# Way down of two of three lots of hidden tiles as seven block products, weight sums by adding transfers, and a third buffer for the second gate/up weight

## The chip, the cores and the metric

The kernel runs on one core of one Trainium2 chip. The metric is the device time of one execution in microseconds (us); the time before is the median of three runs, 1095.49 us (1094.43 to 1097.13). The engines of the core are TensorE (PE: matmuls, its weight loads shown as PEld), VectorE (DVE), ScalarE (ACT), GpSimd (POOL) and SyncE (SP, which issues transfers).

## The reference

Two transformer layers on x of 512 tokens x 1024, in fp32: a token mixer with memory attention, then a gated feed-forward part. The change touches the feed-forward part only:

```
h  = rms_norm(x, g_ffn_pre[i])
gu = h @ w_gate_up[i]                                    # 1024 x (2 * 2816)
f  = (silu(gu[..., :D_FF]) * gu[..., D_FF:]) @ w_down[i]  # 2816 x 1024
x  = x + rms_norm(f, g_ffn_post[i])
```

## The kernel before, in words

**Precision.** Every fp32 factor of a product is held as two numbers, a rounded high part (ACT copies it into the matmul format) and the low remainder (DVE subtracts), made by `split` (L313, L317). A product is then three matmuls: high x high, high x low, low x high (`mm3`, L303 to L305).

**Tiles and lots.** The 2816 hidden columns are 22 tiles of 128 (`NF`), the 512 tokens four row tiles (`NT`). `LOTS` (L44) groups the hidden tiles into three lots: eight, six and eight. For each lot the kernel first makes the hidden tiles (gate/up), then multiplies them with their rows of `w_down` (way down) and adds the result into `o`, four tiles of 128 x 1024 fp32. The third lot's way down is in `ffn_out`, together with the norm that ends the layer.

**Gate/up.** Hidden tiles 0 and 1 of a layer are made plainly (`plain`, `act`). Tiles 2 to 21 go through `body` (L1085): the 512 tokens and the 1024 inputs are halved, and gate and up stand for the two column halves, so that eight block products become seven (Strassen's scheme in Winograd's form). Each of the seven is `seven` (L1059): 4 x 3 matmuls of 256 columns. The token side's sums are made once per layer by `Forms`; the weight side's sums are made for every hidden tile: `prep_a` loads the first weight `ra` and splits it, `load_b` loads the second, `rb`, and makes two sums on DVE (L1043, L1044), `prep_c` makes the third (L1049) and splits `ru`, `prep_b` splits `rb`, `prep_d` adds once more (L1056) and splits 512 columns. Within a tile the products are S2, nS1, S3, S4, A22; the first two of the next tile (`p1`, `p2`: A11, A12) stand between them. DVE also combines the products (L1082, L1101, L1109), multiplies silu(gate) by up (L1115) and splits the hidden tile (L1117 on ACT, L1118 on DVE).

**Way down.** `down` (L896): for each half of 512 output columns and each unit of two hidden tiles, one weight load of 128 x 1024, one split, then 4 row tiles x 2 x 3 matmuls of 512 columns. The first unit's products of row tiles 0 and 1 are issued early, inside the last gate/up tile (`fill`, the functions `first` and `second`), to bridge the time in which that tile is finished. In layer 0 every unit also calls `ahead` (L226): two calls together load and split one weight of layer 1's mixer and store the two parts to memory (14 calls in all, of eight weights asked for).

**Order.** PE's order is the program's. The other engines' and the transfers' order is chosen by a scheduler from what is ready; instructions then run in that order on each engine. A buffer of a pool is handed on when its last reader is done: `raw` has three, `ru` and `rb` two each, the split weights `hi` and `lo` four each. PSUM has eight banks: `acc` two, `s0` to `s2`, `pv`, `t` two. Transfers are issued by SP.

```
LOTS = ((0, 8), (8, 14), (14, 22))
            ru, rb = [gu.tile([P, 1024], F32, tag=z, name=z, bufs=2) for z in ("ru", "rb")]
```

## Time and profile before

| | |
|---|---|
| median of three runs | 1095.49 us |
| profiled execution | 1097.01 us, its span 1094.9 us |
| granted TensorE clock | 0.998 of full |
| transfers | 142.44 MB, of which the queue of SP has 140.80 MB |
| layer 0, feed-forward by blocks | from 222 us to 549 us of the span |
| layer 1, the same | from 776 us to the end |

A row of the profile names a line of the kernel, the engine, the operation, what it writes and reads by the program's names, the shape, and then the busy time in all, the mean time of one in ns, and the idle time of the engine just before, with what ended it. Rows in order of time give the start, the duration, and in brackets an idle time and its end. Matmuls overlap in the pipeline: the duration of one in a row is longer than the distance to the next.

### The profile page before, as it was taken

How to read it: one execution, taken by the hardware profiler on the slowest of the kernel's cores; microseconds unless marked ns; L12 is line 12 of the kernel's file. 1: busy time of each engine (PE TensorE's matmuls, PEld its weight loads, DVE VectorE, ACT ScalarE, POOL GpSimd, SP SyncE). 2: the span in 40 equal slices, each digit the busy share in tenths (PEclk: the TensorE clock that was granted, in tenths of full speed). 3: DMA queues.
4: the chain of work that ended last, by engine and by line, in shares of the span. 5: the costliest groups of instructions: out<-in, count | busy, mean ns of one | idle time of the engine just before them, and what ended most of it. 6: DMA issues, size and time to landing. Idle time of an engine off the chain costs nothing.

```text
span 1094.9 us, 19518 instructions
## 1 busy us (share of the span) xinstructions
PE 1072.8 (98%) x7436; PEld 985.0 (90%) x7436; DVE 840.8 (77%) x1433; ACT 659.1 (60%) x1357; POOL 197.7 (18%) x341
## 2 busy tenths in 40 slices
PE   9999999999999999999999999999999999999997
PEld 7899878999889989998898888878999899899986
DVE  7889875999548867975888988758996478669854
ACT  7679874756445535653567888756664366346631
POOL 5773231102000000000444543312000000000001
PEclk9999999999999999999999999999999999999999
DMA  9621007344833472335533221144136123423243
GB/s 339 250 78 40 20 20 261 125 154 129 283 140 116 153 252 78 116 108 187 197 126 116 78 78 40 39 176 172 53 110 222 59 89 120 139 68 105 88 165 116
DMA packets 40702, 142.44 MB, mean 130 GB/s; under 512 B 4768, under 2 KB 5152, under 8 KB 40480
## 3 DMA queue, kind: packets, MB, share of 16 engines
q1 hardware_dynamic: 40320, 140.80, 37.4%
q8 instruction: 58, 0.95, 0.4%
q10 hardware_dynamic: 288, 0.40, 0.1%
q14 instruction: 36, 0.29, 0.1%
HBM read 122.30 MB, written 18.87 MB: 129 GB/s over the span
## 4 chain that ended last, share of the span: by engine, by line
PE 70%; DVE 5%; issue 2%; ACT 1%; POOL 1%; DMA 0%; DVEq 0%; POOLq 0%; ACTq 0%
PE ps L1065 11%; PE ps L1066 11%; PE ps L1067 11%; PE ps L304 10%; PE ps L303 10%; PE ps L305 10%; PE tp L668 2%; DVE wlo L317 1%; PE o L683 1%; PE o L682 1%; PE s L607 1%; PE s L608 1%; POOL r L337 1%; DVE hrows L317 1%; POOL p L658 0%
## 5 line engine op out<-in xcount | busy, mean ns | idle before, releaser
L313 ACT ACTIVATE whi<-raw 128x1024 fp32r<-128x1024 f32 (+3 forms) x206 | 169.2, 839 | 170.1 <-PE ps L1067 69.0
L317 DVE TENSOR_TENSOR wlo<-raw,whi 128x1024 fp32r<-128x1024 f32 (+3 forms) x202 | 191.0, 960 | 68.8 <-ACT whi L313 64.8
L1066 PE MATMUL ps<-hrows,wlo 128*128 128x256 f32 x640 | 176.4, 276 | 0.0
L1065 PE MATMUL ps<-hrows,whi 128*128 128x256 f32 x640 | 176.2, 275 | 0.0
L1067 PE MATMUL ps<-hrows,whi 128*128 128x256 f32 x640 | 176.2, 275 | 0.0
L303 PE MATMUL ps<-whi,hrows 128*128 128x256 f32 (+2 forms) x432 | 144.1, 333 | 0.0
L304 PE MATMUL ps<-wlo,hrows 128*128 128x256 f32 (+2 forms) x432 | 138.0, 320 | 1.6 <-DVE wlo L317 1.6
L304 PE MATMUL ps<-wlo,f 128*128 128x512 f32 (+1 forms) x360 | 138.6, 385 | 0.0
L303 PE MATMUL ps<-whi,f 128*128 128x512 f32 (+1 forms) x360 | 138.5, 385 | 0.0
L305 PE MATMUL ps<-whi,f 128*128 128x512 f32 (+1 forms) x360 | 138.5, 385 | 0.0
L305 PE MATMUL ps<-whi,hrows 128*128 128x256 f32 (+2 forms) x432 | 138.0, 320 | 0.0
L1065 PE MATMUL ps<-a,whi 128*128 128x256 f32 x480 | 132.3, 276 | 2.9 <-DVE c L1101 2.9
L1066 PE MATMUL ps<-a,wlo 128*128 128x256 f32 x480 | 132.1, 275 | 0.0
L1067 PE MATMUL ps<-a,whi 128*128 128x256 f32 x480 | 132.1, 275 | 0.0
L1066 PEld LDWEIGHTS ps<-hrows,wlo 128*128 128x128 f32 x640 | 120.1, 188 | 0.6
L1065 PEld LDWEIGHTS ps<-hrows,whi 128*128 128x128 f32 x640 | 120.1, 188 | 0.5
L1067 PEld LDWEIGHTS ps<-hrows,whi 128*128 128x128 f32 x640 | 120.1, 188 | 0.0
L346 POOL TENSOR_SCALAR e<-sso 128x1 f32<-128x1 f32 x8 | 3.4, 422 | 550.5 <-ACT junk L341 550.3
L658 POOL TENSOR_SCALAR p<-p,rd 128x256 f32<-128x256 f32 (+2 forms) x128 | 77.4, 623 | 102.5 <-DVE rd L655 62.3
L1065 PEld LDWEIGHTS ps<-a,whi 128*128 128x128 f32 x480 | 90.1, 188 | 3.5 <-DVE c L1101 3.3
L1066 PEld LDWEIGHTS ps<-a,wlo 128*128 128x128 f32 x480 | 90.1, 188 | 0.2
L1067 PEld LDWEIGHTS ps<-a,whi 128*128 128x128 f32 x480 | 90.1, 188 | 0.0
(201 smaller groups left out, 2551.0 us busy)
## 6 DMA issues: line engine op xcount, KB each, us to landing
raw<-in_wgu_dram SPq DMA_DIRECT2D x48, 512.0 KB, 4.4
raw<-in_wd_dram SPq DMA_DIRECT2D x44, 512.0 KB, 4.5
rb<-in_wgu_dram SPq DMA_DIRECT2D x40, 512.0 KB, 3.6
raw<-in_wo_dram SPq DMA_DIRECT2D x17, 512.0 KB, 4.1
raw<-in_wq_dram SPq DMA_DIRECT2D x16, 512.0 KB, 4.9
xt<-x SPq DMA_DIRECT2D x12, 512.0 KB, 4.9
raw<-in_wm_dram SPq DMA_DIRECT2D x8, 512.0 KB, 4.6
x<-y SPq DMA_DIRECT2D x8, 512.0 KB, 3.2
```

The costliest lines, as they stand in the source:

```text
L303: mm(out, lh, rh, start=first, stop=False)
L304: mm(out, lh, rl, start=False, stop=False)
L305: mm(out, ll, rh, start=False, stop=last)
L313: a = nc.scalar.activation(hi, src, AF.Copy)
L317: b = nc.vector.tensor_sub(lo, src, hi.bitcast(F32))
L337: g.tensor_tensor(r, r, self.mhalf[:, :r.shape[1]], op=OP.pow)
L607: nc.tensor.matmul(s[:, :n], qi, hd["ka"]()[:, k0 * P:k1 * P], start=True, stop=False)
L658: self.pooled = nc.gpsimd.tensor_scalar(hd["p"][z][:, :n], hd["p"][z][:, :n], rd[:, z:z + 1], 1.0, op0=OP.mult, op1=OP.mult)
L668: nc.tensor.transpose(tp[:, z], hd["p"][i][:, jj * P:(jj + 1) * P], self.ident)
L1065: mm(out, wh[:, s], rh, start=start and k == 0, stop=False, skip_group_check=True)
L1066: mm(out, wl[:, s], rh, start=False, stop=False, skip_group_check=True)
L1067: mm(out, wh[:, s], rl, start=False, stop=k == 3, skip_group_check=True)
```

## The change

- **Lots.** Six, six and ten hidden tiles. The first two lots use a new `down` inside `ffn`; the third goes through `ffn_out` as before, which now has five units of two tiles: in its second half of columns four are split first, the products of the first unit run for all row tiles, then the fifth is split.
- **Seven block products.** In a lot of six, tokens (2 x 256), hidden tiles (2 x 3) and output columns (2 x 512) are halved: A11, A12, A22, S1, S2, S3, S4 against weight blocks b11, b21, t4, t1, t2, t3, b22. Each product is 3 hidden tiles x 2 row tiles x 3 matmuls of 512 columns. The results are added into `o` by `out_of`: 14 results of 512 columns a lot; in the first lot eight of them are copies on ACT, otherwise DVE adds. The blocks are 768 KB (512 KB and a rest of 256 KB in `rs`, four buffers); `pairs` splits them into two buffers of `hi` and `lo` each. A11 runs inside the last gate/up tile.
- **Hidden sums.** `keep_hidden` makes the token side's sums: the first three tiles of a lot are kept in fp32 (`k`; tiles 0 and 1 in `o`), the last three are combined with them on DVE and split once more.
- **Adding transfers.** `add` is a transfer issued from GpSimd that adds its source to its target. For tiles from the third on in each lot (`far`), the three sums L1043, L1044 and L1049 become a second load of the weight and three adds of 256 KB, the third of which waits for the first. The sums t1 to t4 of the blocks are also loads and adds; t2 uses t1, t4 uses t2. The first two tiles of each lot keep the sums on DVE.
- **Buffers.** `ru` and `rb` have three buffers (`wide`); the third and the temporary tiles are opened after the forms of the layer are closed. Both loads of a tile are now issued with `prep_a`, one tile earlier for `rb`.
- `ahead` is called six times in each way down of the first two lots, 12 in all.

The diff, cut to its core (the packing of the down weights into blocks on the host is left out, as is the split of `ending` into `part`):

```diff
 PLACE = (128, dict(hT=22, th=0, sf=28)), (48, dict(hT=6, th=48, sf=FORM))
-LOTS = ((0, 8), (8, 14), (14, 22))
+LOTS = ((0, 6), (6, 12), (12, 22))
+HALF = 3
...
@@ -893,23 +899,6 @@
             late[t] = lambda t=t, h=h: forms.turn(t, h)
...
-    def down(self, get, w, fs, c, o, head=None):
-
-        nc = self.nc
-        for h in range(2):
-            ps = head["ps"] if h == 0 else [self.tagged(z) for z in ("s", "pv", "acc", "acc")]
-            for u in range(len(fs) // 2):
-                wu = head["w"] if (h, u) == (0, 0) else self.unit(w[h, fs[0] // 2 + u])
-                for t in range(0 if h or u else 2, NT):
-                    self.down_prod(ps[t], get, fs, u, t, wu)
-                self.ahead()
-            for t in range(NT):
-                z = o[t][:, 512 * h:512 * h + 512]
-                if c == 0:
-                    nc.scalar.activation(z, ps[t], AF.Copy)
-                else:
-                    nc.vector.tensor_add(z, z, ps[t])
-
     def down_prod(self, ps, get, fs, u, t, wu):
...
-        wu = [self.unit(w[1, fs[0] // 2 + u]) for u in range(nu)]
+        wu = [self.unit(w[1, u]) for u in range(nu - 1)]
+        ps, tail = [], []
+        for t in range(NT):
...
+                ps.append(self.tagged(("s", "pv", "acc", "acc")[t]))
+                self.down_prod(ps[t], get, fs, 0, t, wu[0])
+        wu.append(self.unit(w[1, nu - 1]))
...
-        def hidden(i):
-            return [f32r(pools["f"], [P, S], f"f{z}{i}") for z in range(2)]
+        def slots(i, n=S):
+            return [f32r(pools["f"], [P, n], f"f{z}{i}") for z in range(2)]
+
+        def signed(pair, c, src):
+            nc.scalar.activation(pair[0][:, c], src, AF.Copy, scale=-1.0)
+            nc.vector.scalar_tensor_tensor(pair[1][:, c], src, -1.0, pair[0][:, c].bitcast(F32), op0=OP.mult,
+                                           op1=OP.subtract)
+
+        def keep_hidden(f, s):
+
+            lot = next(c for c, (f0, f1) in enumerate(LOTS) if f0 <= f < f1)
+            i = f - LOTS[lot][0]
+            p = F[f] = slots(i)
+            a, b = slice(0, 256), slice(256, 512)
+            if lot == len(LOTS) - 1:
+                signed(p, slice(0, 512), s)
+            elif i < HALF:
+                signed(p, a, s[:, a])
+                nc.vector.tensor_sub(s[:, a], s[:, a], s[:, b])
+                signed(p, b, s[:, a])
+                kept[i] = s
+            else:
+                signed(p, slice(0, 512), s)
+                q = i - HALF
+                r = kept.pop(q)
+                x = temp("q")
+                nc.vector.tensor_add(x[:, b], s[:, b], r[:, a])
+                nc.vector.tensor_sub(x[:, a], s[:, b], r[:, b])
+                nc.vector.tensor_sub(r[:, a], s[:, a], x[:, b])
+                F["S12", lot, q] = v = slots(i + HALF)
+                self.split(v[0], v[1], x)
+                if q % 2 == 0:
+                    F["S4", lot, q // 2] = slots(3 * HALF + q // 2, 512 if q < HALF - 1 else 256)
+                signed(F["S4", lot, q // 2], (a, b)[q % 2], r[:, a])
+
+        def block(c, name, z, i, t):
+            f0 = LOTS[c][0]
+            key, h = {"A11": (f0 + i, 0), "S3": (f0 + i, 1), "A12": (f0 + HALF + i, 0), "A22": (f0 + HALF + i, 1),
+                      "S1": (("S12", c, i), 0), "S2": (("S12", c, i), 1), "S4": (("S4", c, i // 2), i % 2)}[name]
+            pair = F[key]
+            return pair[z][:, 256 * h + P * t:256 * h + P * t + P]
...
         def temp(tag, n=512):
-            return tmp.tile([P, n], F32, tag=tag, name=tag, bufs=2 if n == 512 else 1)
+            return tmp.tile([P, n], F32, tag=tag, name=tag, bufs={"c": 2, "s": 2, "k": HALF}.get(tag, 1))
+
+        def product(f):
+            lot = next(c for c, (f0, f1) in enumerate(LOTS) if f0 <= f < f1)
+            if f < 2:
+                return o[2 + f][:, :512]
+            return temp("k" if lot < len(LOTS) - 1 and f - LOTS[lot][0] < HALF else "s")
...
         def act(f, pg):
-            s = temp("s")
+            s = product(f)
             nc.scalar.activation(s, pg[0], AF.Silu)
-            nc.vector.tensor_mul(s, s, pg[1])
-            F[f] = hidden(f)
-            self.split(F[f][0], F[f][1], s)
+            nc.vector.scalar_tensor_tensor(s, s, -1.0, pg[1], op0=OP.mult, op1=OP.mult)
+            keep_hidden(f, s)
...
-        def prep_a(f):
+        def wide(tag):
+            n = turn[tag] = turn.get(tag, -1) + 1
+            return (gx if n % 3 == 2 else gu).tile([P, 1024], F32, tag=tag, name=tag, bufs=1 if n % 3 == 2 else 2)
+
+        def load_a(f):
             st[f] = {}
-            src = self.a["wgu"][l, f]
             ra = self.wraw.tile([P, 1024], F32, tag="raw", name="raw", bufs=3)
-            nc.sync.dma_start(ra, src[0])
+            nc.sync.dma_start(ra, self.a["wgu"][l, f, 0])
             raw[f] = ra
-            pair(f, "a", ra)
-
-        def load_b(f):
-            src = self.a["wgu"][l, f]
-            ru, rb = [gu.tile([P, 1024], F32, tag=z, name=z, bufs=2) for z in ("ru", "rb")]
-            nc.sync.dma_start(rb, src[1])
-            with self.tc.issue_after(forms.last[1]) if f == 3 else nullcontext():
-                nc.vector.tensor_add(ru[:, :512], raw[f][:, :512], rb[:, :512])
-                nc.vector.tensor_add(rb[:, :512], rb[:, :512], rb[:, 512:])
-            st[f].update(ru=ru, rb=rb)
+
+        def add(dst, src):
+            nc.gpsimd.dma_start(dst, src, accum_op=OP.add, max_dma_last_dim=4096)
+
+        def load_b(f, far):
+            sa, sb = self.a["wgu"][l, f, 0], self.a["wgu"][l, f, 1]
+            ru, rb = wide("ru"), wide("rb")
+            nc.sync.dma_start(rb, sb)
+            st[f].update(ru=ru, rb=rb, far=far)
+            if far:
+                nc.sync.dma_start(ru, sb)
+                add(ru[:, :512], sa[:, :512])
+                add(rb[:, :512], sb[:, 512:])
+                add(ru[:, 512:], ru[:, :512])
+
+        def prep_a(f, far):
+            load_a(f)
+            load_b(f, far)
+            pair(f, "a", raw[f])
         def prep_c(f):
             ru, rb = st[f]["ru"], st[f]["rb"]
-            nc.vector.tensor_add(ru[:, 512:], ru[:, :512], rb[:, 512:])
+            if not st[f]["far"]:
+                with self.tc.issue_after(forms.last[1]) if f == 3 else nullcontext():
+                    nc.vector.tensor_add(ru[:, :512], raw[f][:, :512], rb[:, :512])
+                    nc.vector.tensor_add(rb[:, :512], rb[:, :512], rb[:, 512:])
+                nc.vector.tensor_add(ru[:, 512:], ru[:, :512], rb[:, 512:])
             pair(f, "c", ru)
...
-        def body(f, pos, nxt, nxt2, fill):
+        def body(f, nxt, nxt2, fill, begin):
...
             if nxt is not None:
-                load_b(nxt)
                 prep_c(nxt)
                 p1(nxt)
             else:
@@ -1104,7 +1164,9 @@
             else:
                 fill[1]()
             if nxt2 is not None:
-                prep_a(nxt2)
+                prep_a(nxt2, True)
+            elif nxt is not None:
+                begin()
             seven(f, y, "b", 1, "S4", False)
             nc.vector.tensor_add(c[:, :256], y, d["u2"])
...
             nc.vector.tensor_mul(s, s, c)
-            F[f] = hidden(pos)
-            nc.scalar.activation(F[f][0], s, AF.Copy, scale=-1.0)
-            nc.vector.scalar_tensor_tensor(F[f][1], s, -1.0, F[f][0].bitcast(F32), op0=OP.mult, op1=OP.subtract)
+            keep_hidden(f, s)
             if nxt is not None:
                 prep_d(nxt)
...
-        tmp = self.pool(ff, f"ft{l}")
+        turn, temps = {}, ExitStack()
...
         pools["forms"].close()
+        tmp, gx = self.pool(temps, f"ft{l}"), self.pool(temps, f"gx{l}")
+
+        def load_block(main, *src):
+            t = [main, tmp.tile([P, 512], F32, tag="rs", name="rs", bufs=4)]
+            for z, x in enumerate(t):
+                for n, y in enumerate(src):
+                    y = y[z] if isinstance(y, list) else y[:, 1024 * z:1024 * z + x.shape[-1]]
+                    nc.sync.dma_start(x, y) if n == 0 else add(x, y)
+            return t
...
+        def pairs(t):
+            out = []
+            for x in t:
+                n = x.shape[-1]
+                hi, lo = [self.whl.tile([P, 1024], F32R, tag=z, name=f"w{z}", bufs=4) for z in ("hi", "lo")]
+                self.split(hi[:, :n], lo[:, :n], x)
+                out.append((hi, lo))
+            return out
+
+        def times(c, ps, name, pr, steps, fresh):
+            mm = nc.tensor.matmul
+            for i, t in steps:
+                lh, ll = block(c, name, 0, i, t), block(c, name, 1, i, t)
+                rh, rl = [pr[i // 2][z][:, i % 2 * 512:i % 2 * 512 + 512] for z in range(2)]
+                mm(ps[t], lh, rh, start=fresh and i == 0, stop=False, skip_group_check=True)
+                mm(ps[t], lh, rl, start=False, stop=False, skip_group_check=True)
+                mm(ps[t], ll, rh, start=False, stop=i == HALF - 1, skip_group_check=True)
+
+        BY_ROW = [(i, t) for t in range(2) for i in range(HALF)]
...
+        BY_UNIT = [(0, 0), (1, 0), (0, 1), (1, 1), (2, 0), (2, 1)]
...
+        def out_of(c, ps, row, col, fresh, less=False):
+            for t in range(2):
+                z = o[2 * row + t][:, 512 * col:512 * col + 512]
+                if c == 0 and fresh:
+                    nc.scalar.activation(z, ps[t], AF.Copy, scale=-1.0 if less else 1.0)
+                else:
+                    (nc.vector.tensor_sub if less else nc.vector.tensor_add)(z, z, ps[t])
+
+        def down_load(c, h):
+            (b11, b12), (b21, b22) = [[self.a["ws"][l, c, z, n] for n in range(2)] for z in range(2)]
+            h["b11"] = load_block(self.wraw.tile([P, 1024], F32, tag="raw", name="raw", bufs=3), b11)
+            h["t1"] = load_block(wide("ru"), b11, b12)
+            h["b21"] = load_block(wide("rb"), b21)
+            h["t2"] = load_block(wide("ru"), b22, h["t1"])
+            h["t3"] = load_block(wide("rb"), b12, b22)
+
+        def down_begin(c, h):
+            h["x"] = [self.tagged("acc"), self.tagged("acc")]
+            h["w"] = pairs(h["b11"])
+            times(c, h["x"], "A11", h["w"], BY_UNIT[:4], True)
+
+        def down(c, h):
+
+            x, b21, b22 = h["x"], self.a["ws"][l, c, 1, 0], self.a["ws"][l, c, 1, 1]
+            out_of(c, x, 0, 0, True)
+            w = pairs(h["b21"])
+            z = [self.tagged("s"), self.tagged("s")]
+            times(c, z, "A12", w, BY_UNIT, True)
+            h["b22"] = load_block(wide("rb"), b22)
+            out_of(c, z, 0, 0, False)
+            self.ahead()
+            w = pairs(h["t2"])
+            times(c, x, "S2", w, BY_UNIT, False)
+            out_of(c, x, 0, 1, True, True)
+            t4 = load_block(wide("rb"), b21, h["t2"])
+            self.ahead()
+            w = pairs(h["t1"])
+            y = [self.tagged("pv"), self.tagged("t")]
+            times(c, y, "S1", w, BY_ROW, True)
+            out_of(c, y, 1, 1, True)
+            self.ahead()
+            w = pairs(h["t3"])
+            times(c, x, "S3", w, BY_ROW, False)
+            out_of(c, x, 1, 1, False, True)
+            self.ahead()
+            w = pairs(h["b22"])
+            times(c, y, "S4", w, BY_ROW, False)
+            out_of(c, y, 0, 1, False)
+            self.ahead()
+            w = pairs(t4)
+            times(c, x, "A22", w, BY_ROW, False)
+            out_of(c, x, 1, 0, True)
+            self.ahead()
...
             if c:
-                prep_a(gs[0])
-            load_b(gs[0])
+                prep_a(gs[0], False)
             prep_c(gs[0])
-            prep_a(gs[1])
+            prep_a(gs[1], False)
...
+            last = c == len(LOTS) - 1
+
+            def begin():
+                if not last:
+                    down_load(c, head)
             def first():
-                head["w"] = self.unit(self.a["wd"][l][0, f0 // 2])
+                if not last:
+                    down_begin(c, head)
...
+                head["w"] = self.unit(self.a["wd"][l][0, 0])
...
             def second():
+                if not last:
+                    times(c, head["x"], "A11", head["w"], BY_UNIT[4:], True)
+                    return
...
             for i, f in enumerate(gs):
                 more = gs[i + 1:] + [None, None]
-                body(f, f - f0, more[0], more[1], [first, second])
-            if c < len(LOTS) - 1:
-                self.down(get, self.a["wd"][l], fs, c, o, head)
+                body(f, more[0], more[1], [first, second], begin)
+            if not last:
+                down(c, head)
                 if l == c == 0:
-                    self.axial(gu.tile([P, 1024], F32, tag="ru", name="ru", bufs=2))
+                    self.axial(wide("ru"))
+        temps.close()
         done()
         return get, fs, o, head
```

More of the change, by code (lines that the diff above doesn't have):

```diff
@@ L962, in ffn_out @@
         for u in range(nu):
-            wu = head["w"] if u == 0 else self.unit(w[0, fs[0] // 2 + u])
+            wu = head["w"] if u == 0 else self.unit(w[0, u])
             for t in range(0 if u else 2, NT):
@@ L976, in ffn_out @@
                 break
[L977 to L979 removed]
+            for u in range(1, nu):
+                self.down_prod(ps[t], get, fs, u, t, wu[u])
             if rs is not None and t >= 2:
```

44 lines of the change are left out of this document (28 added, 16 removed).

## The prediction, made before the changed kernel was timed

> **What bounds the kernel now.** I read the page's first table, then the waits of TensorE (PE), then the busy time by stage, then single rows in order of time.
>
> ```profile
> span 1094.9 us, 19518 instructions
> PE 1072.8 (98%) x7436; PEld 985.0 (90%) x7436; DVE 840.8 (77%) x1433; ACT 659.1 (60%) x1357; POOL 197.7 (18%) x341
> ...
> PE ps L1065 <- DVE c L1101: 2.9, 2, 2.3
> PE ps L304 <- DVE wlo L317: 1.6, 2, 0.8
> ```
>
> PE is busy nearly throughout, and the longest waits that it has anywhere are a few us in all. By stage (columns: length, busy us and count of PE, PEld, DVE, ACT, POOL, clock, DMA share, GB/s), here layer 0: gate/up of the first lot, its way down, the same of the second, gate/up of the third:
>
> ```profile
> 222.00:284.60 62.60, 60.33 (x518) 59.61 (x517) 55.97 (x80) 35.86 (x62) 7.13 (x7) 1.00 0.51 170
> 284.60:325.40 40.80, 40.80 (x182) 33.80 (x181) 21.79 (x23) 16.54 (x21) 0.00 (x0) 1.00 0.62 212
> 325.40:385.40 60.00, 60.00 (x517) 59.45 (x517) 46.43 (x67) 34.41 (x59) 0.00 (x0) 1.00 0.40 135
> 385.40:415.40 30.00, 30.00 (x135) 24.83 (x135) 22.17 (x27) 11.14 (x12) 0.00 (x0) 1.00 0.60 206
> 415.40:494.50 79.10, 79.10 (x686) 78.56 (x685) 64.74 (x95) 47.15 (x78) 0.00 (x0) 1.00 0.34 108
> ```
>
> PE is busy for the whole of each but the first, which lacks 2.3 us, at the full granted clock of 1.00; VectorE (DVE) has slack, 46.43 of 60.00 us beside gate/up and 22.17 of 30.00 beside the way down. So time falls by what PE no longer has to do, as long as nothing else becomes late.
>
> Busy means overlap, so I take the pace of PE from starts (start, duration, row):
>
> ```profile
> 284.61 0.39 PE L303 MATMUL ps<-whi,f 128*128 128x512 f32 x1
> ...
> 325.44 0.28 PE L1065 MATMUL ps<-a,whi 128*128 128x256 f32 x1
> ```
>
> Way down of the first lot: eight hidden tiles x 4 row tiles x 2 halves x 3 = 192 matmuls, 12 of them already issued inside the last gate/up tile, so 180 in 40.83 us: 0.227 us for one of 512 columns, though its row says 0.39.
>
> **The products on PE.** A lot of six tiles took 6 x 4 x 2 x 3 = 144 matmuls. Seven block products of 3 hidden tiles x 2 row tiles x 3 = 18 make 126. That is 18 less in each of four lots: 72 x 0.227 = **-16.3 us**. The third lot grows from eight to ten tiles, the first shrinks from eight to six: the sum of tiles stays 22, so this costs nothing on PE. In the last row tile of layer 1 the halves of 256 columns grow in number, not in columns: nothing.
>
> **VectorE's load.** Its rows through one gate/up tile of the third lot:
>
> ```profile
> 428.85 0.69 DVE L1115 TENSOR_TENSOR s<-s,c 128x512 f32<-128x512 f32 x1
> 429.45 0.69 DVE L317 TENSOR_TENSOR wlo<-raw,whi 128x512 fp32r<-128x512 f32 x1
> ...
> 431.95 1.23 DVE L317 TENSOR_TENSOR wlo<-ru,whi 128x1024 fp32r<-128x1024 f32 x1 [0.61 <-ACT whi L313]
> 433.09 0.69 DVE L1043 TENSOR_TENSOR ru<-raw,rb 128x512 f32<-128x512 f32 x1
> 433.69 0.42 DVE L1101 TENSOR_TENSOR c<-ps,p 128x256 f32<-128x256 f32 x1
> 434.03 0.68 DVE L1044 TENSOR_TENSOR rb<-rb 128x512 f32<-128x512 f32 x1
> ...
> 438.37 0.69 DVE L1115 TENSOR_TENSOR s<-s,c 128x512 f32<-128x512 f32 x1
> ```
>
> From start to start 1024 columns cost 1.14, 512 cost 0.60, 256 cost 0.34 us; a tile comes every 9.52 us (428.85 to 438.37), with 0.61 us idle. A tile has splits of 3 x 1.14 + 0.60, four sums and two other operations of 512, three of 256: 8.6 us. The change takes three sums (1.80) out of 28 of the 40 tiles: all but the first two of each lot. It adds in the block lots 0.42 us for each of the first three hidden tiles (three operations of 256 for one of 512) and 1.96 us for each of the last three. The heaviest tile whose next one is summed by transfers is 8.6 - 1.80 + 1.96 = 8.8 of 9.52 us. Gate/up stays behind PE: **0**. If that cover went, each tile would cost its excess over 9.52.
>
> In the way down a product now lasts 18 x 0.227 = 4.1 us. It needs a block of 1536 columns split, 1.14 + 0.60 = 1.74 us, and two results of 512 emptied, 1.2 us; in layer 0 half a unit kept for layer 1 besides, 0.57. Sum 3.5 of 4.1: tight. For the second lot of layer 0, from the end of the last gate/up tile to the next lot's first sums: the last tile's hidden work 0.6 + 2.56, six blocks 10.4, 14 results 8.4, three kept units 3.4, the next tile's first split and sums 2.9, together 28.3 us, while PE has 24.5 us of products and 1.4 us of the next tile. That is 2.4 us too much; some of the first results can move into the last gate/up tile. I take **+1.5**, between 0 and 2.4. In the first lot of layer 0, 8 results go to ScalarE (ACT): 23.5 us, no excess; in layer 1 no units are kept: 20.1 and 24.9, none.
>
> **The new wait at the head of the way down.** Block A12 follows the last gate/up product directly. Its weights (hidden rows 4 to 6, first half of the columns) need two of four split buffers, and the first of these is held by the last tile's product S4, which ends 1.36 us (12 matmuls of 256 columns, 9.52 / 84 = 0.113 each) before A12 is due.
>
> ```profile
> L313 ACT ACTIVATE whi<-raw 128x1024 fp32r<-128x1024 f32 x100 | 105.4, 1059 | 158.9 <-PE ps L1067 67.0 <-PE ps L305 56.7 <-DMA pair<-whi 24.2
> L317 DVE TENSOR_TENSOR wlo<-raw,whi 128x1024 fp32r<-128x1024 f32 x100 | 121.8, 1222 | 67.5 <-ACT whi L313 63.7 <-DMA pair<-wlo 2.2
> L1117 ACT ACTIVATE f<-s 128x512 fp32r<-128x512 f32 x40 | 25.2, 631 | 8.9 <-DVE s L1115 8.8
> L1114 ACT ACTIVATE s<-ps 128x256 f32<-128x256 f32 x40 | 15.2, 379 | 10.8 <-PE ps L1067 10.5
> ```
>
> 1.06 + 1.22 = 2.28 us of splitting against 1.36 + 0.23 (A12's first matmul needs only the high half): 0.7 us at least if nothing stands ahead. DVE also has the product of the last hidden tile (0.60) there: 1.3. Until now this place was covered by 12 matmuls of the first unit for the other two row tiles. The last hidden tile itself is first needed four steps, 2.7 us, into A12; its chain is 0.38 + 0.69 + 0.63 + 0.69 = 2.4 us. Bounds 0 (the order saves it) to 2.5 a lot; I take 1.2, near the row sum: four lots, **+4.8**. What queues behind that split on DVE: the hidden tile's low half and the emptying of A11, for which product S2 waits.
>
> **The wait that goes, and what is late next.** The 2.9 us above lie at one place in each layer:
>
> ```profile
> 242.34 0.28 PE L1067 MATMUL ps<-hrows,whi 128*128 128x256 f32 x1
> 244.88 0.39 PE L1065 MATMUL ps<-a,whi 128*128 128x256 f32 x1 [2.27 <-DVE c L1101]
> ...
> 242.66 0.69 DVE L1043 TENSOR_TENSOR ru<-raw,rb 128x512 f32<-128x512 f32 x1 [1.39 <-DMA rb<-in_wgu_dram]
> ```
>
> DVE stood on a late load of rb, with c queued behind it. With a third buffer the load starts earlier and DVE no longer waits for it by itself. But the third buffer opens only when the transposed forms are closed (about 222 us, where the first stage above begins), and the late weights are those of the first tile with adding transfers: two loads, then two adds one behind the other. The tile before it starts 72 matmuls (8.2 us) ahead of 242.5, and the split of the sums stands in the queues of ACT and DVE from its first two products on, at 237 us, with c behind it. Adds are not in this trace; their neighbours are (bytes moved, KB of one, us to landing; for the queue packets, MB, share of 16 engines):
>
> ```profile
> q1 hardware_dynamic: 40320, 140.80, 37.4%
> ...
> raw<-in_wgu_dram SPq DMA_DIRECT2D x48, 512.0 KB, 4.4
> ...
> xT<-in_xT_dram SPq DMA_DIRECT2D x8, 256.0 KB, 5.3
> ...
> smem<-mT SPq DMA_DIRECT2D x1, 2048.0 KB, 8.9
> ...
> out_dram<-o SPq DMA_DIRECT2D x2, 256.0 KB, 2.0
> ```
>
> An add of 256 KB lies between a plain 256 KB (2.0) and the largest transfer seen (8.9): the chain takes 4.4 + 2 x 2.0 = 8.4 to 4.4 + 2 x 8.9 = 22.2 us, against 15: from -2.9 (both waits go) to +7. I take **0**: near the 5.3 of the same size, 15.0 us. In the steady state three buffers give two tiles and 2.7 us, 21.8 us, so latency is hidden.
>
> The Trainium skill, "DMA: Bandwidth & Descriptors", section "Anatomy of one DMA — SWDGE (gpsimd) path", fits 2.0 us + bytes / 436e3 to a transfer issued by GpSimd, an estimated 2.6 us for 256 KB. By it the chain would be 9.6 us and the term -2.9. No run here shows such a transfer.
>
> Transfers are not held to their place in the program:
>
> ```profile
> L698 SPq DMA_DIRECT2D ru<-in_ropeb_dram x1: 328/328/328, 261.7 to 261.7; - x1
> L705 POOL TENSOR_TENSOR gt<-ru x4: 455/916/1442, 269.1 to 272.3; 128x128 f32<-128x128 f32 x4
> ```
>
> This load is written behind the first way down (after 325 us) and issued at 261.7. So the blocks' loads start when their buffers come free; their 8 issues on POOL and 0.33 us each on SP stand beside idle queues (POOL 0.00 busy in those stages), except for this axial table, some 7 us once.
>
> **Kept units.** The way down of layer 0 now asks 12 times instead of 14, so six units are kept for layer 1, not seven; one more split of 1.06 and 1.22 us in layer 1's mixer, which isn't PE's bound everywhere: **+0.3**, 0 to 1.2.
>
> **Sum.** -16.3 + 4.8 + 1.5 + 0 + 0.3 = -9.7 us. The profiled run took 1097.0 us (span 1094.9 and 2.1 around it), so 1087.3 for a run like it; it lay 1.5 above the median of 1095.5, so **1085.8**. With the terms' bounds this case spans 1079 to 1092.
>
> **Rivals.** *All of it is kept* (no wait at A12, the 2.9 us go too): 1095.5 - 16.3 = 1079.2, down to 1076.3. For it: the splits and hidden work have room in the last gate/up tile, where DVE has nothing to prepare. Against: the buffer held by S4. Chance 0.18.
>
> *VectorE becomes the bound of the way down.* If each of the seven splits also leaves 0.61 us of idle time behind ACT, as in the row at 431.95, a lot needs 4.3 us more: excesses 6.7, 1.9 and 3.3 us in the two lots of layer 0 and the second of layer 1. 11.9 us in place of 1.5 leaves +0.7: about 1096. Chance 0.09.
>
> *Adding is slow: the other sign.* Place: the third lot, eight tiles in a row. 140.80 MB in 37.4% of 1094.9 us is 0.344 MB per us. A tile loads 3 x 0.524 MB, 4.57 us, and adds 0.786 MB at k times a plain byte's time, 2.29k us. At k = 2 it is 9.1 of 9.52 us; above 2.16 DMA is slower than PE. At k = 3 it is 11.4, 1.9 us late a tile, less some 6.5 us a lot that the first two tiles (plain, 3.05 us) leave: 8.8 + 1.1 us a layer, 19.8 in both: 1105.6. The sign turns near k = 2.8. Blocks add to it in layer 0, where DMA is already at 0.62. For it: an add must read its target too, and the row shows only plain ones. Against: DMA idles 60 to 66% of the gate/up stages of the second and third lot. Chance 0.15.
>
> *POOL's issues are held up by VectorE.* In the L705 row one shape takes 455 to 1442 ns on POOL. If three issues a tile each lose 1 us, a chain of 22.2 grows to 25.2 us, 11.0 us a tile over 2.29 tiles in flight; 1.5 x 8 - 6.5 = 5.5 us a layer: 1097. Chance 0.03. The Trainium skill, "SBUF — State Buffer", section "SBUF: two separate sides", says that DVE in its two-port mode keeps GpSimd from writing descriptors; it names fp32 copies, while DVE's rows here are operations on two tensors. No run here shows it.
>
> **How the numbers follow.** My forecast has 0.55. A measurement of this kernel tells about 0.3%, 3.3 us. Faster: 0.55 + 0.18 = 0.73; same 0.09 + 0.03 = 0.12; slower 0.15. The range, 1077 to 1100, takes in the first three cases and the fourth, and the nearer part of slow adding; about 0.15 is left out.
>
> **What would show it.** Right: 984 matmuls' worth of 512 columns at the way down's lines in place of 1056 (22 tiles x 24 x 2 layers); in the waits, PE behind DVE's or ACT's split at the start of each block way down, about 1 us, four times; no L1043 sums from the third tile of a lot on; tiles still every 9.52 us. Wrong: PE waiting for splits behind DMA in the third lot, or DVE above 95% through a way down. The prediction falls if tiles come slower than 9.6 us, or if the way down of a block lot takes over 29 us beyond its last gate/up tile.

## The result, and the profile after

| | before | after |
|---|---|---|
| median of four runs | 1096.31 us (1094.43 to 1098.24) | 1135.47 us (1134.44 to 1143.23) |
| profiled execution, its span | 1097.01 us, 1094.9 us | 1134.44 us, 1132.6 us |
| granted TensorE clock | 0.998 | 0.983 |

The ratio is 1.0372, with a 95% interval of 1.0322 to 1.0422: 39 us slower, where 9.7 us faster was forecast. (One execution each of two experiments below took over 3,600 us with the whole program stretched; they are left out.)

The page of the changed kernel, its first table and its two large queues (packets, MB, share of 16 engines):

```profile
span 1132.6 us, 20097 instructions
PE 1075.4 (95%) x7370; PEld 978.9 (86%) x7370; DVE 857.2 (76%) x1491; ACT 691.2 (61%) x1427; POOL 298.1 (26%) x457
...
q1 hardware_dynamic: 48816, 164.39, 41.9%
q0 software_dynamic: 16704, 34.61, 18.1%
```

PE's share fell from 98% to 95%, so PE waits. The adding transfers are q0: 34.61 MB in 18.1% of 1132.6 us are 0.169 MB per us, where q1 has 0.346. A byte added took 2.05 times a byte of the plain transfers.

The waits of PE in the changed kernel (us in total, times, longest):

```profile
PE ps L1233 <- DVE wlo L323: 13.1, 11, 4.0
PE ps L1232 <- ACT whi L319: 12.6, 5, 7.9
PE ps L1126 <- DVE c L1161: 10.8, 2, 5.8
```

L1232 and L1233 are the block products, L1126 the gate/up products: both kinds wait, for halves of weights and for c, 36.5 us in these three groups. Before, the largest group of the feed-forward parts had 2.9. By stage, in the columns used above. Layer 0: each lot of six with its way down, the gate/up of the third lot, and two of that lot's tiles; then the two lots of six of layer 1:

```profile
221.00:307.00 86.00, 74.32 (x479) 66.25 (x478) 66.53 (x98) 46.84 (x77) 17.99 (x22) 0.94 0.91 257
307.00:409.00 102.00, 90.18 (x617) 81.29 (x616) 74.31 (x114) 50.91 (x86) 19.28 (x22) 0.93 0.90 249
409.00:507.00 98.00, 98.00 (x852) 97.43 (x851) 74.23 (x103) 59.84 (x99) 18.45 (x21) 1.00 0.77 197
...
439.00:458.00 19.00, 19.00 (x171) 19.00 (x169) 14.35 (x20) 12.02 (x21) 5.31 (x6) 1.00 1.00 250
...
801.00:887.00 86.00, 73.48 (x464) 65.05 (x463) 61.69 (x95) 44.33 (x74) 15.08 (x17) 0.94 0.88 251
887.00:976.00 89.00, 86.92 (x635) 81.28 (x634) 74.77 (x116) 50.06 (x85) 16.89 (x19) 1.00 0.79 208
```

The third lot, where slow adding was feared, loses nothing: PE is busy 98.00 of 98.00 us even while the DMA engines are full (1.00 in the row of its two tiles). The loss is in the lots of six: in layer 0 PE lacks 11.7 and 11.8 us, the granted clock is 0.94 and 0.93, and DMA is at 0.91 and 0.90, where the same part of the old kernel had 0.40 to 0.62. In layer 1 the first lot lacks 12.5 us, the second only 2.1.

To count all of PE's lost time I take every distance between the starts of two neighbouring matmuls, less 0.227 us for 512 columns, 0.114 us for 256, and for other widths in proportion. It is 64.5 us before and 118.4 after: +53.9. Less the 16.3 us of products that are gone this gives 37.6; the spans differ by 37.7. Of the 53.9, 33.0 lie in layer 0's feed-forward part, 20.8 in layer 1's (each from its first block product of gate/up to its last product of the way down). By lots of six, in order, the changed kernel loses 17.5, 17.9, 19.1 and 2.5 us. Three kinds of place hold most of it.

**The first tile with adds.** From the timeline of the changed kernel (start, duration, engine, row; the brackets give an idle time and its end):

```profile
222.77 1.24 SPq L1094 DMA_DIRECT2D ru<-in_wgu_dram  x1
...
228.57 0.87 POOL L1086 DMA_DIRECT2D ru<-in_wgu_dram  x1
...
237.40 0.87 POOL L1086 DMA_DIRECT2D ru<-ru  x1 [6.65 <-DMA ru<-in_wgu_dram]
...
245.16 0.69 DVE L1117 TENSOR_TENSOR raw<-raw,ru 128x512 f32<-128x512 f32 x1 [7.01 <-DMA ru<-ru]
...
247.87 0.42 DVE L1161 TENSOR_TENSOR c<-ps,p 128x256 f32<-128x256 f32 x1
...
248.34 0.58 PE L1126 MATMUL ps<-a,whi 128*128 128x256 f32 x1 [5.82 <-DVE c L1161]
```

Load, add, second add: 5.8 + 8.8 + 7.8 = 22.4 us from the load's issue to its use. DVE stood for it, c stood behind that on DVE, and PE waited 5.82 us; with what follows PE lost 7.7 us here and 7.4 at the same place of layer 1 (2.4 and 0.8 in the old kernel).

**A11, inside the last gate/up tile.** The same timeline, later:

```profile
356.07 1.06 ACT L319 ACTIVATE whi<-raw 128x1024 fp32r<-128x1024 f32 x1
...
356.96 0.43 DVE L1037 TENSOR_TENSOR q<-s,k 128x256 f32<-128x256 f32 x1
...
359.18 0.42 DVE L1016 SCALAR_TENSOR_TENSOR f<-k,f 128x256 fp32r<-128x256 f32 x1
359.51 1.22 DVE L323 TENSOR_TENSOR wlo<-raw,whi 128x1024 fp32r<-128x1024 f32 x1
...
360.78 0.52 PE L1233 MATMUL ps<-wlo,f 128*128 128x512 f32 x1 [2.08 <-DVE wlo L323]
```

ACT had the high half at 357.13; DVE came to the low half at 359.51, after six operations of the hidden sums. The block had landed before, so it is the order on DVE. The wait stands four times, once at 4.00 us and three times at 2.08.

**The last block product.** Its block t4 ends with an add of 512 columns:

```profile
393.26 0.86 POOL L1086 DMA_DIRECT2D ru<-ru  x1 [6.95 <-DMA ru<-in_wgu_dram]
393.81 1.21 POOL L1086 DMA_DIRECT2D rs<-rs  x1
...
403.14 0.63 ACT L319 ACTIVATE whi<-rs 128x512 fp32r<-128x512 f32 x1 [11.28 <-DMA rs<-rs]
...
403.82 0.79 PE L1232 MATMUL ps<-whi,f 128*128 128x512 f32 x1 [7.88 <-ACT whi L319]
```

In GpSimd's queue the add of the rest (`rs`) stands behind an add for the next lot's tile, which held the queue for 6.95 us until its own target was there; then the rest took 9.3 us to be usable. With the slow clock behind it the place lost 10.7 us. The way down of this lot is seen between the last gate/up product and the next:

```profile
370.45 0.28 PE L1128 MATMUL ps<-a,whi 128*128 128x256 f32 x1
...
409.19 0.28 PE L1126 MATMUL ps<-a,whi 128*128 128x256 f32 x1
```

38.7 us; the four ways down take 27.4, 38.7, 33.0 and 24.9.

### The profile page after: what moved, and what is told of

Read it like the earlier page. It is cut to its first block, busy times and chain, and to the rows that moved or that the text cites. A ratio compares the mean times of both kernels' runs of the same rounds, so it can differ in the third digit from the quotient of the medians.

```text
span 1132.6 us, 20097 instructions
## 1 busy us (share of the span) xinstructions
PE 1075.4 (95%) x7370; PEld 978.9 (86%) x7370; DVE 857.2 (76%) x1491; ACT 691.2 (61%) x1427; POOL 298.1 (26%) x457
## 3 DMA queue, kind: packets, MB, share of 16 engines
q1 hardware_dynamic: 48816, 164.39, 41.9%
q0 software_dynamic: 16704, 34.61, 18.1%
## 5 line engine op out<-in xcount | busy, mean ns | idle before, releaser
L319 ACT ACTIVATE whi<-raw 128x512 fp32r<-128x512 f32 (+3 forms) x188 | 149.8, 815 | 117.7 <-PE ps L1128 50.8
L323 DVE TENSOR_TENSOR wlo<-raw,whi 128x1024 fp32r<-128x1024 f32 (+3 forms) x184 | 168.2, 929 | 54.3 <-ACT whi L319 54.0
L1126 PE MATMUL ps<-hrows,whi 128*128 128x256 f32 x640 | 177.5, 277 | 0.9 <-ACT p L1132 0.9
L1126 PE MATMUL ps<-a,whi 128*128 128x256 f32 x480 | 133.8, 279 | 10.8 <-DVE c L1161 10.8
L1128 PE MATMUL ps<-a,whi 128*128 128x256 f32 x480 | 133.4, 278 | 0.0
L1126 PEld LDWEIGHTS ps<-hrows,whi 128*128 128x128 f32 x640 | 121.1, 189 | 1.9 <-ACT p L1132 1.3
L1126 PEld LDWEIGHTS ps<-a,whi 128*128 128x128 f32 x480 | 91.2, 190 | 11.5 <-DVE c L1161 11.2
L1128 PEld LDWEIGHTS ps<-a,whi 128*128 128x128 f32 x480 | 91.3, 190 | 0.0
L310 PEld LDWEIGHTS ps<-wlo,hrows 128*128 128x128 f32 x432 | 81.5, 189 | 7.1 <-DVE wlo L323 2.2
L1086 POOL DMA_DIRECT2D ru<-ru x32 | 27.8, 870 | 222.6 <-DMA ru<-in_wgu_dram 190.0
L309 PEld LDWEIGHTS ps<-whi,hrows 128*128 128x128 f32 x432 | 81.4, 188 | 5.4 <-ACT whi L319 0.6
L311 PEld LDWEIGHTS ps<-whi,hrows 128*128 128x128 f32 x432 | 81.2, 188 | 5.2
```

Source lines behind the costliest of these rows:

```text
L309: mm(out, lh, rh, start=first, stop=False)
L310: mm(out, lh, rl, start=False, stop=False)
L311: mm(out, ll, rh, start=False, stop=last)
L319: a = nc.scalar.activation(hi, src, AF.Copy)
L323: b = nc.vector.tensor_sub(lo, src, hi.bitcast(F32))
L1086: nc.gpsimd.dma_start(dst, src, accum_op=OP.add, max_dma_last_dim=4096)
```

## The experiments

Theory T: the adding transfers crowd the lots of six; what waits there is late because each add costs two bytes' time and stands in one queue. Rival V: VectorE, with the hidden sums and the splits, became the bound. Rival O: the transfers are fine, a few places are in a bad order. The expectations of runs 1 to 8 split theory T in two: L, the adds come late; B, their bytes fill the DMA engines. Times are medians; each ratio is to runs of the old kernel on the same chip (1095.5 to 1096.3).

**1. `e1_tile_sums_dve`: the tiles' sums back on VectorE.**

```diff
-                prep_a(nxt2, True)
+                prep_a(nxt2, False)
```

> The changed kernel with the gate/up weight sums of every tile made on VectorE again, so that only the block sums of the way down are made by adding transfers; third buffer, lots and block products stay. Theory L (late adds: an add lands 6 to 10 us after its issue and GpSimd issues them one after the other, so the first tile with adds in each layer and block t4 come late, and TensorE's clock falls after each such wait): the 7.7 and 7.4 us at the first such tile fall to the 2 to 3 us of before, and the 10.7 and 4.7 us at t4 vanish because no tile's add stands ahead of t4's on GpSimd: some 25 us less, about 1110 us. Rival V (VectorE is the bound in the block lots): VectorE gets 1.8 us more in 28 tiles, so the time rises, over 1140 us. Rival B (the transfers' bytes fill the 16 engines in the block lots): 22 MB of adds less, a partial gain, 1115 to 1125 us.

1117.26 us, 1.0197 [1.0167, 1.0227]. Both first-tile waits and t4's wait are gone; A11's stay (3.3, 2.1, 2.2 and 2.1 us). With all sums on VectorE new waits for its low halves appear, in the third lot:

```profile
PE ps L1127 <- DVE wlo L323: 5.8, 10, 1.1
```

So the tiles' adds cost 18 us more than they bring, though in the third lot they bring something: it loses 6.0 and 4.9 us here in the two layers, next to nothing in the changed kernel.

**2. `e2_block_sums_out`: the blocks' adds left out** (the sums t1 to t4 are missing from the result; their loads stay).

```diff
-                    nc.sync.dma_start(x, y) if n == 0 else add(x, y)
+                    if n == 0:
+                        nc.sync.dma_start(x, y)
```

> The changed kernel with the adds of the block sums t1 to t4 left out (each block is only loaded, so the sums are missing from the result); the gate/up tiles keep their adding transfers. Theory L: the wait at block t4 (10.7 and 4.7 us with the lowered clock) and the 2.3 us at 868 us vanish, the two waits at the first tile with adds stay, and the waits at A12 stay: about 1118 us. Rival V: unchanged, 1132 to 1136 us, since VectorE does the same work. Rival B: 12.6 MB of adds less, in the stages where DMA is fullest: also a gain, but spread over all waits of these stages, A12 and the first tile with adds included.

1115.59 us, 1.0182 [1.0152, 1.0211]. t4's waits go; the first tile's (5.0 and 3.3) and A11's (4.0, 2.1, 2.1, 2.1) stay. Taking either kind of add away gives back 18 to 20 us.

**3. `e3_adds_in_order`: adding transfers issued in the order of the program.**

```diff
-            nc.gpsimd.dma_start(dst, src, accum_op=OP.add, max_dma_last_dim=4096)
+            with self.tc.issue_after(adds[-1]) if adds else nullcontext():
+                adds.append(nc.gpsimd.dma_start(dst, src, accum_op=OP.add, max_dma_last_dim=4096).ins)
```

> The changed kernel with all adding transfers issued by GpSimd in the order in which the program writes them, so that t4's adds go ahead of the next lot's tile adds; the work and the bytes are the same. Theory L: t4's rest lands before its split is due and the 10.7 and 4.7 us go or shrink to 0 to 3; the first tile with adds and A12 keep theirs: 1119 to 1127 us. Rivals B and V: same bytes and same VectorE work, so 1132 to 1137 us.

1121.51 us, 1.0236 [1.0164, 1.0308]. t4's wait of 7.88 is gone, but one of 2.7 us comes in the first lot's way down, and the first tile's (5.9, 4.2) and A11's stay. The order explains one place only.

**4. `e4_adds_alone`: the old lots and the old way down, with the adding transfers for the tiles and the third buffer.**

```diff
-LOTS = ((0, 6), (6, 12), (12, 22))
+LOTS = ((0, 8), (8, 14), (14, 22))
...
-                down(c, head)
+                self.down(get, self.a["wd"][l], fs, c, o, head)
```

> The kernel before with one part of the change alone: gate/up weight sums by adding transfers from the third tile of a lot on and the third buffer; lots of eight, six and eight and the old way down. Theory L: only the wait at the first tile with adds is left, 7 to 8 us in each layer against about 3 and 1 of before: 1096 + 11 = 1107 us. Rival V or a loss by the block products themselves: this part is free or helps, 1092 to 1097 us.

1101.72 us, some 6 us over the old kernel: a single time, from which no more than the sign follows. The third buffer was not tried by itself.

**5. `e5_split_first`: the first block's split ahead of the hidden work.**

```diff
-            h["w"] = pairs(h["b11"])
+            with self.urgent():
+                h["w"] = pairs(h["b11"])
```

> The changed kernel with one thing of order altered: the two splits of block b11 (for product A11, inside the last gate/up tile of a block lot) are given priority, so that VectorE makes their low halves ahead of the hidden sums of the tile before; same work. Theory O (A11's wait of 2.08 to 4.0 us in each of the four block lots is VectorE's order: its low half was made last of nine operations, 2.4 us after its high half was there): the four waits and the slowed clock behind three of them, 5.9 + 4.0 + 2.4 + 2.4 = 14.6 us, go: about 1121 us. Rival V (VectorE has too much to do there in any order): the wait moves to the hidden sums and A12, time stays within 5 us of 1135.

1123.73 us, 1.0247 [1.0198, 1.0296]. All four A11 waits are gone, so VectorE's order was their cause. With the slow clock behind them they lose 14.6 us in the profile of the changed kernel; 11.7 us come back in the medians and 9.2 in the profiled spans, as waits elsewhere grow (the first tile's to 6.2 and 5.3 us). This edit stays in the runs 8 to 17.

**6. `e6_first_tile_dve`, 7. `e7_t4_on_dve`, 8. `e8_three_together`: the other two places mended, alone and with run 5.**

```diff
-                prep_a(nxt2, True)
+                prep_a(nxt2, nxt2 != 4)
...
-            t4 = load_block(wide("rb"), b21, h["t2"])
+            t4 = [wide("ru"), h["b21"][1]]
+            for z in range(2):
+                nc.vector.tensor_add(t4[z], h["b21"][z], h["t2"][z])
```

> The changed kernel with the weight sums of one tile per layer (the fifth, the first one that has adds) made on VectorE; all other adds stay. Theory L: the waits there, 7.7 and 7.4 us with the slowed clock, fall to 1 to 3 us, nothing else changes much: 1122 to 1126 us. Rival B (bytes): 0.8 MB of 34.6 less, no change, 1133 to 1136 us.

> The changed kernel with the sum t4 made on VectorE from b21 and t2, which lie in the core already, in place of a load of 768 KB and an add of 768 KB in each block lot. Theory L: the waits at the last block, 10.7 and 4.7 us, go: about 1120 us. Rival V: VectorE gets 1.7 us more in each way down, so the time stays at 1135 or rises.

> The three alterations together: b11 split first, the fifth tile of each layer summed on VectorE, t4 summed on VectorE. Theories L and O: the three gains add up, 1135 - 14.6 - 12 - 15.4 = 1093 us, which leaves some 12 us of other waits against the 16 us that TensorE saves. Rival V: little of it, 1120 us or more.

1131.45 us (1.0318 [1.0279, 1.0356]), 1138.65 (1.0383 [1.0309, 1.0458]) and 1121.66 (1.0228 [1.0156, 1.03]). All three missed what theory L expected. Runs 7 and 8 came out as rival V had it, run 6 between its two outcomes. With tile 4 summed on VectorE the wait stands at tile 5; the timeline of run 6 has

```profile
255.86 0.58 PE L1126 MATMUL ps<-a,whi 128*128 128x256 f32 x1 [4.48 <-DVE c L1161]
```

and in run 7 t4 is on time but waits of up to 5.5 us stand at earlier blocks. Mending these places moved the wait to the next one: against rival O, which run 5 had borne out at A11 alone.

**9. `e9_adds_left_out`, 10. `e10_copies_for_adds`: run 5 with no adding transfers at all, and with plain copies from the same queue in their place** (the sums are missing from both results).

```diff
-            nc.gpsimd.dma_start(dst, src, accum_op=OP.add, max_dma_last_dim=4096)
+            return
```

```diff
-            nc.gpsimd.dma_start(dst, src, accum_op=OP.add, max_dma_last_dim=4096)
+            nc.gpsimd.dma_start(dst, src)
```

> The kernel with b11 split first, and every adding transfer left out (tiles and blocks are loaded as before, the sums are missing from the result, and VectorE doesn't make them either). Revised theory T (adding transfers are the cause, since with one late place mended the wait moved to the next tile with adds: they take the engines' time and their chain is long in the short block lots): all waits but a few us go, 1123.7 - 44 + 6 = about 1086 us, with TensorE's 16 us to be seen for the first time. Rival V (the block products cost VectorE and ACT too much): 1110 us or more.

> As the run with the adds left out, but each add is a plain copy of the same bytes from the same queue of GpSimd, with the same waits (the sums are missing from the result). If it is what an add costs the transfer engines beyond a copy (34.6 MB took 205 us of 16 engines, 0.169 MB per us, where SP's queue made 0.346), the time lies near the run without adds, 1088 to 1098 us. If it is the chain of issues and waits on GpSimd, whatever the transfer does, it lies near 1124 us.

1083.34 us (0.988 [0.9842, 0.9918]) and 1097.93 (1.0013 [0.9987, 1.0039]). Without adds the gain of the block products is there: PE's lost time is 67.8 us, 3.3 above the old kernel's, and the 16.3 - 3.3 = 13.0 us that this leaves show in the time. The added plain loads (SP's queue moves 164.39 MB where it moved 140.80) are in this run too, so they are not the cause. Rival V falls for the work that VectorE has in the changed kernel: it does the same in this run as in run 5. That it has no room for more at the ways down is what runs 7, 12 and 17 show. The same transfers as copies cost 14.6 us, as adds another 25.8. GpSimd's queue in run 10, and landings there (KB each, median us):

```profile
q0 software_dynamic: 10304, 34.61, 9.1%
...
rb<-in_wgu_dram POOLq DMA_DIRECT2D x28, 256.0 KB, 4.4
ru<-in_wgu_dram POOLq DMA_DIRECT2D x28, 256.0 KB, 4.8
```

and in the changed kernel:

```profile
rb<-in_wgu_dram POOLq DMA_DIRECT2D x28, 256.0 KB, 7.4
ru<-in_wgu_dram POOLq DMA_DIRECT2D x28, 256.0 KB, 8.1
ru<-ru POOLq DMA_DIRECT2D x28, 256.0 KB, 6.0
```

9.1% of 1094.2 us for 34.61 MB are 0.348 MB per us: as fast as SP's queue. The copies went out in 10304 packets, the adds in 16704, so the runs don't separate adding itself from its smaller packets.

**11. `e11_adds_third_lot`: run 5, with the tiles' sums by transfer in the third lot only. 12. `e12_third_lot_t4_dve`: that, with t4 as in run 7.**

```diff
-                prep_a(nxt2, True)
+                prep_a(nxt2, nxt2 >= LOTS[-1][0])
```

> b11 split first, and tiles' weight sums by adding transfers in the third lot alone; in the two block lots VectorE makes them, block sums stay adds. Theory T: the block lots lose their waits on tile adds (as in the run with all tile sums on VectorE, 1117.3 us), A11's four waits go (-12 to -16), and the third lot keeps VectorE free (its 9 us of small waits in that run go): 1090 to 1097 us. Rival V: VectorE is too full in the block lots, 1108 us or more.

> As the run with adds for tiles in the third lot alone, and t4 made on VectorE from what lies in the core: 1.5 MB less to transfer in each block lot, 1.7 us more for VectorE. Theory T: the same or up to 4 us faster. Rival V: slower by 3 to 7 us.

1104.06 us (1.0071 [1.0051, 1.0092]) and 1108.67 (1.0111 [0.9998, 1.0225]). Run 11 keeps the tiles' adds in the third lot and drops those in the lots of six: 19.7 us better than run 5. In run 11 one large wait is left, again t4's rest behind a tile's add:

```profile
377.81 0.86 POOL L1086 DMA_DIRECT2D ru<-ru  x1 [6.44 <-DMA ru<-in_wgu_dram]
378.36 1.21 POOL L1086 DMA_DIRECT2D rs<-rs  x1
...
388.37 0.79 PE L1232 MATMUL ps<-whi,f 128*128 128x512 f32 x1 [7.52 <-ACT whi L319]
```

The whole of t4 on VectorE is no cure. In run 12 its sum stands on VectorE, after idle time, ahead of the first block's low half, and PE waits for that at the head of the way down, in layer 0 and likewise (3.4 us) in layer 1:

```profile
256.07 1.23 DVE L1277 TENSOR_TENSOR ru<-rb,ru 128x1024 f32<-128x1024 f32 x1 [3.40 <-issue]
...
260.55 0.50 PE L1233 MATMUL ps<-wlo,f 128*128 128x512 f32 x1 [3.54 <-DVE wlo L323]
```

**13. `e13_block_sums_pool`: run 11, with t1, t2 and t4 summed by GpSimd itself.**

```diff
-            h["t1"] = load_block(wide("ru"), b11, b12)
+            h["t1"] = load_block(wide("ru"), b12)
+            for z in range(2):
+                nc.gpsimd.tensor_tensor(h["t1"][z], h["t1"][z], h["b11"][z], op=OP.add)
```

> Tile sums added by transfer in the third lot only, low half of the first block's split placed first, and the block sums t1, t2 and t4 made by GpSimd as tensor operations, t3 still by an adding transfer. If the adding transfers of the blocks are what is left, 1088 to 1093 us, with the wait of 10.5 us at the last block of layer 0's second lot gone. If GpSimd's own work beside VectorE takes their place, VectorE's operations of 512 columns grow from 0.69 towards 1.2 us there and the time stays at 1098 to 1110.

1121.06 us, 1.0229 [1.0188, 1.027]. The second outcome, and larger than expected. A sum on GpSimd, and a split on VectorE that meets it:

```profile
258.02 2.37 POOL L1281 TENSOR_TENSOR ru<-rb,ru 128x1024 f32<-128x1024 f32 x1 [3.27 <-issue]
...
258.47 3.01 DVE L323 TENSOR_TENSOR wlo<-rb,whi 128x1024 fp32r<-128x1024 f32 x1
```

The split takes 3.01 us in place of 1.22.

**14. `e14_t4_rest_dve`: run 11, with only the rest of t4 on VectorE. 15. `e15_order_third_lot`: run 11 with the edit of run 3. 16. `e16_order_and_rest`: both. 17. `e17_rests_dve`: run 14, with the rests of t1 and t2 on VectorE too.**

```diff
-            t4 = load_block(wide("rb"), b21, h["t2"])
+            t4 = [wide("rb"), h["b21"][1]]
+            nc.sync.dma_start(t4[0], b21[:, :1024])
+            add(t4[0], h["t2"][0])
+            nc.vector.tensor_add(t4[1], t4[1], h["t2"][1])
```

> The same third-lot adds and the first block's split placed first; of t4 the rest of 512 columns is summed on VectorE in place of an adding transfer, its main part stays an add. If the late add of that rest is the whole of what is left, the wait of 10.5 us goes and the time is 1092 to 1095 us. If the place is late for any add (the main part's too), the wait stays above 5 us and the time at 1100 or more.

> The same third-lot adds and the first block's split placed first; all adding transfers are issued in the order of the program. If GpSimd's queue order is the cause (the rest of t4 behind the next lot's tile add, which waits for its load), 1093 to 1097 us. If the adds themselves are too long, 1102 us or more, with waits at other blocks.

> Third-lot adds only, the first block's split placed first, the rest of t4 summed on VectorE, and the adding transfers issued in program order. If GpSimd's queue still holds blocks back, 1090 to 1093 us, faster than the old kernel. If what is left are short waits for splits on VectorE and ScalarE, 1095 to 1098, no change.

> Third-lot adds only, the first block's split placed first, and the rests (512 columns) of t1, t2 and t4 all summed on VectorE, the main parts by adding transfers. If the remaining adds cost the time, 1090 to 1094 us. If VectorE is as tight by then, its two more operations of 0.6 us a lot, behind loads, make waits for its low halves: 1097 to 1102.

| run | us | ratio |
|---|---|---|
| 14 | 1096.16 | 0.9999 [0.9989, 1.0009] |
| 15 | 1097.65 | 1.001 [0.9999, 1.0021] |
| 16 | 1095.30 | 0.9991 [0.9981, 1.0001] |
| 17 | 1098.64 | 1.0022 [1.0012, 1.0032] |

Either edit takes the late rest of t4 away, and 6.4 to 7.9 us with it; so GpSimd's order was the cause at that place. The two together bring nothing more, and more sums on VectorE cost again (its low halves hold PE for 4.5 us in all at L1233 in run 17, 1.7 in run 14). The best version, run 16, ties with the old kernel. Its profiled span is 10.4 us above run 9's (1092.3 and 1081.9): PE loses 6.3 us more in layer 0's feed-forward part and 4.9 in layer 1's, in waits of at most 2.1 us for splits and sums. No single cause of that remainder was found.

## Why the prediction was wrong

- **Products on PE, -16.3: right.** Run 9 shows it.
- **VectorE's load, 0: right for the third lot** (tiles every 9.52 us, PE busy 98.00 of 98.00). **VectorE in the way down, +1.5: small, as forecast.** Run 9, without adds, loses 0.8 us in that way down, the second of layer 0, and 2.2 us in the first, where none was forecast.
- **The wait at the head, +4.8: a size and a place off.** It was put at A12, by a split buffer held by S4; it stood one product earlier, at A11, by VectorE's order, and cost 14.6 us there, over the upper bound of 4 x 2.5. The step took it for settled that A11's split would be made in time, and counted only one of the operations queued on VectorE.
- **The first tile with adds, 0: wrong.** The price of an add was taken at 5.3 us, from a plain transfer of the same size; the adds took 8.8 and 7.8. The chain of 22.4 us lies at the upper bound that the prediction had worked out (22.2). And that bound of +7 was counted for one layer where the place comes in two: 7.7 + 7.4 us were lost, 11.9 more than before.
- **Kept units, +0.3: right within its bounds** (between the two feed-forward parts PE loses about 1 us more).
- **The rival of slow adding had the direction, not the place.** It was weighed at the third lot, with a sign that turns at k = 2.8. At the measured k of 2.05 a tile there needs 4.57 + 2.29 x 2.05 = 9.3 of 9.52 us, and it holds. (The 6.5 us credited to the first two tiles there is what one of them leaves, 9.52 - 3.05; the lot holds with either.) The same sum was not made for a lot of six. By the sizes in the front part the second lot of layer 0 loads 16 tile weights of 0.524 MB (8.4), seven blocks of 0.786 (5.5) and moves nine parts of kept units (4.7): 18.6 MB, 54 us at 0.344 MB per us. It adds 4 x 0.786 for tiles and as much for blocks: 6.3 MB, 18.3 us x k. PE has 6 x 9.52 + 126 x 0.227 = 85.7 us. At k = 1 that is 72 us; at 2.05 it is 91.5, and from k = 1.73 on DMA is slower than PE. The windows of the result bear this out: share times length is 92 us there (0.90 of 102.00). The first lots have fewer tiles, and 78 and 76 us of DMA beside some 67 us of products. These three lots lose 17.5 to 19.1 us; the second lot of layer 1, which keeps no units, has 70 beside 86 and loses 2.5.
- **This is the step that failed:** the adding transfers of the lots of six stand in the sum with 0. The first tile's 0 rested on too low a price of an add, and the sentence "Blocks add to it in layer 0, where DMA is already at 0.62" named the load and put no number on it. In its place runs 5, 10 and 9 show 40.4 us: 14.6 for the transfers as copies, 25.8 for adding.
- **Not in the prediction at all:** that an add waiting for its target holds up every add behind it in GpSimd's queue (10.7 us lost at t4 in layer 0), and that a wait is followed by a slow clock (below). Its own test said that it falls if a block way down takes over 29 us; two took 38.7 and 33.0.

The DMA engines' time by lot is not the whole account. Run 11 bears it out in the first lots: there DMA falls from some 75 us each in run 5 to 63 and 60 (0.86 of 72.80, 0.84 of 71.10), and PE loses 10.4 and 13.3 us less than in run 5. But in the second lot of layer 0 the sum, without the tiles' adds and their extra loads, gives 48 + 9.2 x 2.05 = 67 of 85.7 us, and PE still loses 13.5 us, as in run 5 (13.1): most of what is left there is t4's late rest, the order that runs 14 to 16 mend. In run 2 the first lot of layer 0 has 60 us of DMA (0.71 of 84.90) and loses 18.0 all the same, at the first tile and at A11. So an add can come late where the DMA engines have room.

## What to carry to other kernels

Make the transfers' sum for each stage, the most crowded first, with adding transfers at twice a plain byte's time until a run says otherwise. Work that is moved from an idle-looking engine to a queue inherits the order of that queue: look at what an instruction waits for, and at what is then stuck behind it. When a mended wait reappears at the next place, take load away before mending more places.

## What the runs showed of the hardware

**An add costs two copies.** 0.169 MB per us against 0.348 from the same queue. The Trainium skill, "DMA: Bandwidth & Descriptors", section "Rules for kernel authors", says that an accumulating transfer reads its destination and writes it later; the doubled time agrees with that, but packets were smaller too. The estimate of 2.6 us that the prediction worked out from that page for 256 KB lies far below the medians of the tiles' transfers of this size: 6.0 to 8.1 us for adds in the changed kernel, 4.4 to 4.8 for copies in run 10.

**A wait costs more than its length.** Of the 57.0 us that PE loses in the two feed-forward parts after the change, some 38 are waits; the other 19 lie behind them, in a halved clock and in restarting. Windows of the changed kernel after two waits of 2.08 us, the one at 360.78 and the one at 942.60:

```profile
362.00:364.00 2.00, 2.00 (x6) 1.63 (x5) 0.00 (x0) 0.00 (x0) 0.00 (x0) 0.50 1.05 410
```

```profile
942.00:944.00 2.00, 1.41 (x6) 1.19 (x7) 1.15 (x2) 0.00 (x0) 0.00 (x0) 1.00 1.02 213
```

The clock is 0.50 behind the one and 1.00 behind the other. The Trainium skill, "TensorE: Matmul & The Clock Gate", section "What's actually happening", lets the clock drop after an idle window of about 3.4 us that runs freely. The waits of 5.82 and 7.88 us agree; that one of 2.08 us was enough does not. Why the other wait of 2.08 us left the clock alone was not tested.

**GpSimd and VectorE stand in each other's way.** In run 13 a split grew from 1.22 to 3.01 us beside a sum on GpSimd. The Trainium skill, "SBUF — State Buffer", section "SBUF: two separate sides", has the two engines share a pair of ports that one of them holds for a whole instruction, also where VectorE reads two operands; the row agrees.
